# Third layer's query layout, reciprocals and one block's transposes in a four-layer decoder trunk

## The chip, the cores and the metric

The kernel runs on one core of a Trainium2 chip. The metric is the time of one execution on the device in microseconds; the lower, the better. Five engines work side by side, each through its own queue in order: TensorE (PE in the profile; its weight loads are PEld), VectorE (DVE), ScalarE (ACT), GpSimd (POOL) and SyncE (SP), which here only issues DMAs.

## The reference

Four decoder layers over one residual stream of 256 tokens by 1024 channels, all float32. Each layer adds a token mixer's output and then a squared-ReLU MLP's output to the stream, each behind an RMS norm. Layers 0 and 3 use differential attention, layer 1 block-sparse attention (with 256 tokens that is one causal block) and layer 2 sliding-window attention with sinks. What the change touches is layer 2, cut to what matters:

```python
qkv = h @ w_in + b_in                       # 1024 -> 16*64 (q) + 2*64 (k) + 2*64 (v)
q = apply_partial_rope(q.reshape(B, S, 16, 64), cos, sin) * 64 ** -0.5
s = einsum('bnqkgd,bnjkd->bnkgqj', qb, k2)  # 2 key heads, 8 query heads to each, 128 queries a block
s = where(band mask, s, -inf)               # a key is seen for 128 steps
m = maximum(max(s), sink)
e = exp(s - m)
p = e / (sum(e) + exp(sink - m))
o = einsum('bnkgqj,bnjkd->bnqkgd', p, v2)
return o @ w_out
```

Query head h and query head h + 8 belong to key heads 0 and 1.

## The kernel before

**Numbers as pairs.** Matmuls run in the fp32r type. A float32 operand is split into a high part (`whi`, `hg`, `uu`, `oo`: a copy into fp32r) and a low part (`wlo` and the second half of the others: the number less its high part), and three products out of four are summed. Weights come by DMA in pieces of 128x2048 (`fetch`, L173), and `stage` (L185) makes the pair of each: two copies of 128x1024 on ACT (L194) and two subtractions of 128x1024 on DVE (L195). Pieces are staged two ahead of use. Activations stay in the transposed layout (channels on partitions), the stream in `hT0` to `hT3`.

**A layer.** `mixer_layer` (L669) projects with `proj` into PSUM banks `p_in`, makes heads, and leaves the heads' outputs in `parts` (`oo`). `out_proj_all` (layers 0, 2, 3; tiles `p_d`) or `out_proj` (layer 1; tiles `p_d` and `p_e`) multiplies by the output weights and adds to the stream (`into`, L815), which also makes the next norm's pairs (`norm_part`, L345). `up_proj` (L866, tiles `p_up`) takes 16 weight pieces; for each, two banks are filled, copied out by ACT (`cross`, L812), added on DVE (`relu`, L813), squared (L890) and split (L892, L893). `down_proj` (tiles `p_down`, `p_last` in the last layer) closes the layer. In the first three layers, behind the second piece of `up_proj`, the norm's factor comes from GpSimd's sum over partitions (`row`, L387), a scaling (L393) and a DVE reciprocal of 128x256 (L1035).

**Layer 2's mixer.** Keys and values are projected first (L681). Then four pieces of query columns follow, c = 0 to 3. A piece holds 256 columns: two heads of the lower half and the two heads eight further on. Its columns lie lower half first, so that the eviction (L693 to L699) takes four DVE operations of 128x128 for a piece, each of which puts two heads into their places beside their partners in `qn`. After the rotary embedding (`rope`, L437) two blocks are run from a piece, each with one pair of heads; eight blocks in all, called 0 to 7 below. A block (`head_block`, L600) does:
- `scores` (L450): six matmuls into two banks `p_s`; four DVE operations that mask and negate and find the row maximum (`ns`, L473); four exponentials on ACT with row sums (`e` and `l`, L476), two more for the sinks (`es`, L479), and the sums added (L482);
- two DVE reciprocals (L606, L607) and one multiplication of 128x768 by them (L609);
- six transposes of 128x128 on TensorE against the identity (`p_t`, L137), copied to `et` by two ACT operations (L492);
- eight matmuls against the values (`p_av`), copied and split into `oo` (L621, L622).

Layer 1 uses the same `head_block`, and for four of its blocks `turned_aside` (L495): one DVE 32x32 transpose of 128x768 into `squares` (L500) and sixteen GpSimd copies of 32x192 (L504) that put the squares in place. There TensorE has no transposes for the block.

**What sets the order.** A scheduler orders each engine's queue. `TURNS` (L40) adds, by layer, pairs of TensorE instructions counted by tile name: the first of a pair is put behind the second in TensorE's queue. `behind` does the same for two instructions of any engine. PSUM tiles of the tag `wk` (`p_s`, `p_t`, `p_av`, `p_qk`, `p_up`) share four banks in turn, so a new one waits until the bank's last readers are done.

Of the kernel before, what the change touches and what calls it, by code (L numbers as in the profile page):

```python
# [19 lines left out]
P = 128  # L20
# [5 lines left out]
HD = 64  # L26
# [4 lines left out]
FAR = 5  # L31
WARM = 10
RAW = 4
ASIDE_HEADS = (0, 2)
ASIDE_PAIRS = (0,)
ASIDE = (0, 1, 2, 4)
# [49 lines left out]
    2: (  # L86
        (("p_qk", 0), ("p_in", 108)),
        (("p_s", 0), ("p_in", 149)),
        (("p_s", 12), ("p_in", 193)),
        (("p_av", 0), ("p_in", 227)),  # L90
        (("p_s", 36), ("p_d", 46)),
        (("p_s", 45), ("p_d", 60)),
        (("p_s", 42), ("p_d", 55)),
        (("p_d", 150), ("p_d", 161)),
    ),
    3: (
        (("p_s", 0), ("p_in", 83)),
# [54 lines left out]
def trunk(ctx: ExitStack, tc: tile.TileContext, xT, gains, lams, swa_row, fng, weights, out):  # L152
# [284 lines left out]
    def rope(x, nsub):  # L437

        ta = sb.tile([P, NT, nsub, 16], F32, tag="ropea", name="ropea")
        tb = sb.tile([P, NT, nsub, 16], F32, tag="ropeb", name="ropeb")  # L440
        V.tensor_tensor(ta, x[:, :, :, 0:16], cc[:, :, None, :].to_broadcast([P, NT, nsub, 16]), op=OP.mult)
        V.tensor_tensor(tb[:, :, :, 0:8], x[:, :, :, 8:16],
                        nsn[:, :, None, :].to_broadcast([P, NT, nsub, 8]), op=OP.mult)
        V.tensor_tensor(tb[:, :, :, 8:16], x[:, :, :, 0:8],
                        sn[:, :, None, :].to_broadcast([P, NT, nsub, 8]), op=OP.mult)
        V.tensor_tensor(x[:, :, :, 0:16], ta, tb, op=OP.add)

    scored, turned = [0], [0]

    def scores(q, k, mask, sinks):  # L450


        p0, p1 = bank("wk", "p_s0"), bank("wk", "p_s1")
        (qh, ql), (kh, kl) = q, k
        for p, t, n in ((p0, 0, P), (p1, 1, S)):
            o = p[:, :2 * n].rearrange("p (h m) -> p h m", h=2)
            a = slice(P * t, P * t + P)
            mm3(o, qh[:, a], ql[:, a], kh[:, :, :n], kl[:, :, :n], True, True)
        out = []
        if sinks is not None:  # L460
            es = tiny.tile([P, 2 * NT], F32, tag="es", name="es", bufs=2)
        scored[0] += 1
        pair_e = room(4 + scored[0] % 2, [P, 2, 3 * P], "e")
        ls = tiny.tile([P, 2 * NT], F32, tag="l", name="l", bufs=5)
        for c in range(2):
            ns = sb.tile([P, 3 * P], F32, tag="ns", name="ns", bufs=2)
            nm = tiny.tile([P, NT], F32, tag="nm", name="nm", bufs=4)
            l = ls[:, NT * c:NT * c + NT]
            e = pair_e[:, c]
            mk = mask[:, :, :].rearrange("p a b -> p (a b)")  # L470
            for t, p, n in ((0, p0, P), (1, p1, S)):
                s = slice(0, P) if t == 0 else slice(P, 3 * P)
                V.tensor_tensor_reduce(ns[:, s], p[:, n * c:n * c + n], mk[:, s], op0=OP.add, op1=OP.min,  # L473
                                       scale=-1.0, scalar=3.0e38 if sinks is None else sinks[c][1],
                                       accum_out=nm[:, t:t + 1])
                A.activation(e[:, s], ns[:, s], AF.Exp, bias=nm[:, t:t + 1], scale=-1.0,  # L476
                             accum_out=l[:, t:t + 1])
            if sinks is not None:
                A.activation(es[:, NT * c:NT * c + NT], nm, AF.Exp, bias=sinks[c][0])  # L479
            out.append((e, l))  # L480
        if sinks is not None:
            V.tensor_tensor(ls, ls, es, op=OP.add)  # L482
        return out, pair_e, ls
# [11 lines left out]
    def turned_aside(pair_e, h):  # L495

        turned[0] += 1
        ts = room((6, 7, 12, 13)[turned[0] % 4], [P, 2, 3 * P], "et")
        z = room(16 + h % 2, [P, 2, 3 * P], "squares")
        V.transpose(z.rearrange("p c m -> p (c m)"), pair_e.rearrange("p c m -> p (c m)"))  # L500
        to, at = (x.rearrange("p c (j i m) -> p (c j) i m", j=3, m=32) for x in (ts, z))
        for g in range(4):
            for i in range(4):
                G.tensor_copy(to[32 * i:32 * i + 32, :, g, :], at[32 * g:32 * g + 32, :, i, :])  # L504
        return [ts[:, i] for i in range(2)]
# [94 lines left out]
    def head_block(parts, q, k, v, mask, sinks, b, aside=False):  # L600

        _, both_e, l = scores(q, k, mask, sinks)

        rl = tiny.tile([P, 2, 3], F32, tag="rl3", name="rl3")
        l = l.rearrange("p (c t) -> p c t", c=2)
        V.reciprocal(rl[:, :, 0:2], l)  # L606
        V.reciprocal(rl[:, :, 2:3], l[:, :, 1:2])  # L607
        e = both_e.rearrange("p c (j m) -> p c j m", j=3)
        V.tensor_tensor(e, e, rl[:, :, :, None].to_broadcast([P, 2, 3, P]), op=OP.mult)  # L609
# [12 lines left out]
        V.tensor_tensor(both[:, 1], p[:, :S], f(both[:, 0]), op=OP.subtract)  # L622
        parts.append(both)
# [45 lines left out]
    def mixer_layer(i, n):  # L669
# [4 lines left out]
        if mixer == 2:  # L674
# [8 lines left out]
            for t in range(NT):  # L683
                V.scalar_tensor_tensor(kv[:, t, :], p[t], r[:, t:t + 1], rest[:, :256],
                                       op0=OP.mult, op1=OP.add)
            rope(kv[:, :, 0:P].rearrange("p t (s e) -> p t s e", e=HD), 2)
            put_k(kpad, turn(lambda b, t: kv[:, t, 0:P], 1), 1, False)
            kT = [x[:, 0] for x in kpad]
            first, second = [], []
            for c in range(4):  # L690
                p = proj(n, (256, 1), False, first)
                qn = room(c % 2, [P, NT, 256], "qn")
                for t in range(NT):  # L693
                    for h in range(2):
                        s = slice(P * h, P * h + P)
                        o = qn[:, t, :].rearrange("p (b h e) -> p b h e", h=2, e=HD)[:, :, h, :]
                        bs = bias[:, 512 * h + P * c:512 * h + P * c + P]
                        V.scalar_tensor_tensor(o, p[t][:, s].rearrange("p (b e) -> p b e", e=HD), r[:, t:t + 1],
                                               bs.rearrange("p (b e) -> p b e", e=HD), op0=OP.mult, op1=OP.add)  # L699
# [14 lines left out]

                first, second = [lambda f=block: f(0)], [lambda f=block: f(1)]
# [132 lines left out]
    def out_proj(parts, n, rest):  # L848
# [197 lines left out]
    T.take_turns(tc)  # L1046


def weight_pieces(arr):

    out = []
# [4 lines left out]
    for i in range(DEPTH):  # L1056
# [68 lines left out]
```

## Time and profile before

| | us |
|---|---|
| median of 3 runs | 1127.28 |
| lowest and highest run | 1126.79, 1131.32 |
| the profiled execution | 1127.19 |
| its span, first to last instruction | 1125.4 |
| PE busy | 1118.3 |
| PE weight loads busy | 974.8 |
| DVE busy | 840.3 |
| ACT busy | 652.3 |
| POOL busy | 136.6 |

The span is what the profile shows from the first to the last instruction; 1.79 us of the execution lie outside it. A matmul's end is modelled in this profile and matmuls overlap, so single durations of PE are longer than the time from one to the next; the chain of waits, which merges matmuls in order of time, gives their pace. Layer 2's mixer and output projection lie between 581 and 657 us, layer 1's `up_proj` between 403 and 492 us.

### The profile page before, as it was taken

What the parts mean: (1) busy time and instruction counts of PE and PEld (TensorE: products, weight loads), DVE (VectorE), ACT (ScalarE), POOL (GpSimd) and SP (SyncE); (2) the same over time, 40 slices, a digit from 0 to 9 for tenths busy, and PEclk for the clock granted to TensorE, in tenths of its full rate; (3) what the DMA queues carried; (4) which work ended last, traced back from release to release, by engine and by line L of the source; (5) the groups of instructions that cost most, each with busy time, mean ns of one, the idle gap of its engine ahead of it and who ended that gap; (6) DMA issues with size and microseconds to landing.
All of it is one profiled execution on the core that took longest, in us unless ns stands there. A gap on an engine that the chain in (4) does not pass through costs nothing.

```text
span 1125.4 us, 17122 instructions
## 1 busy us (share of the span) xinstructions
PE 1118.3 (99%) x6478; PEld 974.8 (87%) x6478; DVE 840.3 (75%) x1609; ACT 652.3 (58%) x1183; POOL 136.6 (12%) x273
## 2 busy tenths in 40 slices
PE   9999999999999999999999999999999999999997
PEld 7889888888888888888899998888888899888886
DVE  8888977656687798766569888765568788878453
ACT  7776666544476666554446765554446676555342
POOL 2250000000145200000000000000012410002800
PEclk9999999999999999999999999999999999999999
DMA  9533555555544446555563346555554444654551
GB/s 331 203 132 132 191 208 195 191 188 188 178 159 150 149 152 223 189 187 188 187 211 113 113 151 225 187 187 188 187 187 150 154 146 153 221 188 169 187 187 38
DMA packets 30466, 198.67 MB, mean 177 GB/s; under 512 B 3504, under 2 KB 5040, under 8 KB 7216
## 3 DMA queue, kind: packets, MB, share of 16 engines
q1 hardware_dynamic: 30096, 197.09, 50.6%
q8 instruction: 51, 0.84, 0.3%
q10 hardware_dynamic: 288, 0.49, 0.1%
q14 instruction: 31, 0.25, 0.1%
HBM read 196.52 MB, written 1.05 MB: 176 GB/s over the span
## 4 chain that ended last, share of the span: by engine, by line
PE 97%; DVE 1%; issue 1%; DMA 0%; SPq 0%; ACT 0%; POOLq 0%; POOL 0%; DVEq 0%
PE p_up L134 32%; PE p_down L134 24%; PE p_in L134 19%; PE p_last L134 7%; PE p_d L134 7%; PE p_s L134 3%; PE p_av L134 2%; PE p_qk L137 1%; PE p_t L137 1%; PE p_e L134 1%; DMA raw<-in_weights 0%; DVE wlo L195 0%; PE p_o L137 0%; DVE hg L352 0%; DVE acc L361 0%
## 5 line engine op out<-in xcount | busy, mean ns | idle before, releaser
L195 DVE TENSOR_TENSOR wlo<-raw,whi 128x1024 fp32r<-128x1024 f32 (+1 forms) x374 | 451.1, 1219 | 180.6 <-ACT whi L194 180.1
L194 ACT ACTIVATE whi<-raw 128x1024 fp32r<-128x1024 f32 (+1 forms) x374 | 383.8, 1045 | 200.3 <-issue 112.9
L134 PE MATMUL p_up<-hg,whi 128*128 128x512 f32 x1024 | 355.2, 394 | 0.0
L134 PE MATMUL p_up<-hg,wlo 128*128 128x256 f32 x1024 | 283.0, 277 | 0.0
L134 PE MATMUL p_down<-uu,whi 128*128 128x512 f32 x768 | 266.4, 394 | 0.0
L134 PEld LDWEIGHTS p_up<-hg,whi 128*128 128x128 f32 x1024 | 191.8, 188 | 44.0
L134 PE MATMUL p_down<-uu,wlo 128*128 128x256 f32 x768 | 212.7, 277 | 0.0
L134 PE MATMUL p_in<-whi,hg 128*128 128x512 f32 (+1 forms) x736 | 211.3, 370 | 0.0
L134 PEld LDWEIGHTS p_up<-hg,wlo 128*128 128x128 f32 x1024 | 192.3, 188 | 0.4
L134 PEld LDWEIGHTS p_down<-uu,whi 128*128 128x128 f32 x768 | 144.0, 188 | 33.4
L134 PEld LDWEIGHTS p_in<-whi,hg 128*128 128x128 f32 x736 | 132.3, 189 | 24.0 <-DVE hg L352 1.2
L134 PEld LDWEIGHTS p_down<-uu,wlo 128*128 128x128 f32 x768 | 144.2, 188 | 0.0
L134 PE MATMUL p_in<-wlo,hg 128*128 128x512 f32 (+1 forms) x368 | 130.1, 368 | 0.1
L892 ACT ACTIVATE uu<-u 128x512 fp32r<-128x512 f32 x64 | 40.4, 632 | 80.2 <-DVE u L890 80.2
L134 PE MATMUL p_d<-oo,whi 128*128 128x256 f32 (+1 forms) x416 | 85.2, 296 | 0.0
L134 PE MATMUL p_last<-whi,uu 128*128 128x512 f32 (+1 forms) x264 | 79.4, 383 | 0.0
L134 PEld LDWEIGHTS p_in<-wlo,hg 128*128 128x128 f32 x368 | 68.8, 189 | 11.5 <-DVE wlo L195 0.5
L812 ACT ACTIVATE cross<-p_up 128x256 f32<-128x256 f32 x128 | 47.9, 374 | 35.5 <-PE p_up L134 34.1
L134 PEld LDWEIGHTS p_d<-oo,whi 128*128 128x128 f32 x416 | 66.3, 191 | 1.9 <-issue 0.2
L351 ACT ACTIVATE hg<-hT,gn 128x256 fp32r<-128x256 f32 x64 | 31.4, 503 | 60.5 <-DVE hT L825 60.5
L476 ACT ACTIVATE e<-ns,nm 128x128 f32<-128x128 f32 (+1 forms) x128 | 56.8, 446 | 13.8 <-DVE nm L473 13.8
L518 POOL MEMSET kpadh<- 64x512 f32 x8 | 4.2, 521 | 494.3 <-PE p_down L134 494.1
(179 smaller groups left out, 1235.1 us busy)
## 6 DMA issues: line engine op xcount, KB each, us to landing
raw<-in_weights SPq DMA_DIRECT2D x181, 1024.0 KB, 4.9
raw<-in_weights SPq DMA_DIRECT2D x8, 256.0 KB, 4.8
raw<-in_weights SPq DMA_DIRECT2D x4, 512.0 KB, 7.0
hT<-in_xT SPq DMA_DIRECT2D x8, 128.0 KB, 4.7
bias<-in_swa_row SPq DMA_DIRECT2D x1, 512.0 KB, 4.2
grow<-in_fng SPq DMA_DIRECT2D x1, 512.0 KB, 3.8
lv<-in_lams SPq DMA_DIRECT2D x1, 256.0 KB, 6.6
out<-given ACTq DMA_DIRECT2D x1, 256.0 KB, 2.7
```

The lines of the kernel that those rows point to most:

```text
L134: return self.keep(out.tensor.name.rstrip("_0123456789"), self.engine.matmul(out, *args, **kw))
L137: return self.keep(out.tensor.name.rstrip("_0123456789"), self.engine.transpose(out, *args, **kw))
L194: high = A.activation(hi[:, s], raw[:, s], AF.Copy)
L195: low = V.tensor_tensor(lo[:, s], raw[:, s], f(hi[:, s]), op=OP.subtract)
L351: A.activation(both[:, 0], h, AF.Copy, scale=g)
L476: A.activation(e[:, s], ns[:, s], AF.Exp, bias=nm[:, t:t + 1], scale=-1.0, accum_out=l[:, t:t + 1])
L518: G.memset(f(kpad[x][HD * (1 - h):HD * (1 - h) + HD, :, h, :]), 0.0)
L812: A.activation(cross, p[:, S:], AF.Copy)
L892: A.activation(both[:, :, 0], r3(2)(u), AF.Copy)
```

## The change

1. **Query columns by head pairs.** The host lays the query weights and their bias out so that a head of the lower half and its partner stand side by side (`by_pairs`). A piece's eviction is then two DVE operations of 128x256, and in the first piece they are put behind the keys' rotary embedding.
2. **One reciprocal a block** in layer 2. The row sums go to two fixed tiles of 128x32 that are set to 1 at the start; an operand that reads the second and third value twice lets one reciprocal of 128x8 write all the factors.
3. **Block 4 of layer 2** (the fifth) is turned by `turned_aside`, in the block's own step.
4. **Turns.** Layer 2's list of turns is written anew (56 entries for 8), layer 1 gets two more. In the built program TensorE's order differs from before in few places: block 4's six transposes are gone; three output-projection matmuls stand earlier, ahead of block 5's transposes; one matmul of block 4's scores stands a little later; in the last output-projection piece of layer 2 the order of `p_d1` and `p_d3` is changed; and in layer 1 the last four matmuls of `up_proj`'s first piece stand behind five more of the second piece than before.
5. **Layer 1's last output tile** (`p_e` of the fourth) takes its high-weight product as two matmuls of 128x256 instead of one of 128x512, eight times.
6. `turned_aside` takes the two `squares` buffers the other way round.

The scheduler moves some DVE and ACT instructions with this. In layer 1's `up_proj`, the norm factor's scaling and reciprocal stand ahead of the first `relu` addition instead of behind it. In layer 2, ACT has the two copies of a block's transposes behind the next block's exponentials, and DVE has another order around blocks 4 to 7.

```diff
+ASIDE_THIRD = (4,)
...
 TURNS, layer 1:
         (("p_s", 18), ("p_in", 144)),
+        (("p_up", 28), ("p_up", 41)),
+        (("p_up", 30), ("p_up", 29)),
...
+    sink_sums = [cst.tile([P, 32], F32, name=f"sums{x}") for x in range(2)]
+    for x in sink_sums:
+        G.memset(x, 1.0)
...
-        ls = tiny.tile([P, 2 * NT], F32, tag="l", name="l", bufs=5)
+        if sinks is None:
+            ls = tiny.tile([P, 2 * NT], F32, tag="l", name="l", bufs=5)
+        else:
+            ls = sink_sums[scored[0] % 2][:, :2 * NT]
...
-        z = room(16 + h % 2, [P, 2, 3 * P], "squares")
+        z = room(17 - h % 2, [P, 2, 3 * P], "squares")
...
-        rl = tiny.tile([P, 2, 3], F32, tag="rl3", name="rl3")
-        l = l.rearrange("p (c t) -> p c t", c=2)
-        V.reciprocal(rl[:, :, 0:2], l)
-        V.reciprocal(rl[:, :, 2:3], l[:, :, 1:2])
+        rl = tiny.tile([P, 2, 4], F32, tag="rl3", name="rl3")
+        if sinks is None:
+            l = l.rearrange("p (c t) -> p c t", c=2)
+            V.reciprocal(rl[:, :, 0:2], l)
+            V.reciprocal(rl[:, :, 2:3], l[:, :, 1:2])
+        else:
+            V.reciprocal(rl.rearrange("p c (a b) -> p c a b", a=2),
+                         bass.AP(tensor=l.tensor, offset=l.offset, ap=[l.ap[0], [NT, 2], [1, 2], [1, 2]]))
         e = both_e.rearrange("p c (j m) -> p c j m", j=3)
-        V.tensor_tensor(e, e, rl[:, :, :, None].to_broadcast([P, 2, 3, P]), op=OP.mult)
+        V.tensor_tensor(e, e, rl[:, :, :3, None].to_broadcast([P, 2, 3, P]), op=OP.mult)
         es = [both_e[:, c] for c in range(2)]
-        yield
-        ets = turned_aside(both_e, b) if aside else transposed(es)
+        if aside and sinks is not None:
+            ets = turned_aside(both_e, b // 2)
+            yield
+        else:
+            yield
+            ets = turned_aside(both_e, b) if aside else transposed(es)
...
                 for t in range(NT):
-                    for h in range(2):
-                        s = slice(P * h, P * h + P)
-                        o = qn[:, t, :].rearrange("p (b h e) -> p b h e", h=2, e=HD)[:, :, h, :]
-                        bs = bias[:, 512 * h + P * c:512 * h + P * c + P]
-                        V.scalar_tensor_tensor(o, p[t][:, s].rearrange("p (b e) -> p b e", e=HD), r[:, t:t + 1],
-                                               bs.rearrange("p (b e) -> p b e", e=HD), op0=OP.mult, op1=OP.add)
+                    made = V.scalar_tensor_tensor(qn[:, t, :], p[t], r[:, t:t + 1], bias[:, 256 * c:256 * c + 256],
+                                                  op0=OP.mult, op1=OP.add)
+                    if c == 0:
+                        behind(tc, made.ins, roped.ins)
...
-                        h,
+                        h, h in ASIDE_THIRD,
...
+        if "H" in which:
+            for h in range(2):
+                T.matmul(r3(2)(p)[:, h], hi, x[:, h], start=start and h == 0, stop=False, skip_group_check=True)
...
-                    block_step(p, hi[:, k, P * b:P * b + P], lo[:, k, P * b:P * b + P], parts[k], k == 0, k == 7)
+                    block_step(p, hi[:, k, P * b:P * b + P], lo[:, k, P * b:P * b + P], parts[k], k == 0, k == 7,
+                               "Hl" if j and b else "hl")
...
+def by_pairs(x):
+    return np.moveaxis(x.reshape(*x.shape[:-1], 2, 8, HD), -3, -2).reshape(x.shape)
...
+            q = by_pairs(wi[:, :1024])
             for c in range(4):
-                rows(np.concatenate([wi[:, 512 * h + P * c:512 * h + P * c + P] for h in range(2)], axis=1))
+                rows(q[:, 256 * c:256 * c + 256])
```

More of the change, by code (lines that the diff above doesn't have):

```diff
@@ L84 @@
         (("p_s", 18), ("p_in", 144)),
-    ),
-    2: (
-        (("p_qk", 0), ("p_in", 108)),
[L88 to L94, printed above, removed]
+        (("p_up", 28), ("p_up", 41)),
+        (("p_up", 30), ("p_up", 29)),
+    ),
+    2: (
+        (("p_in", 109), ("p_qk", 1)),
+        (("p_qk", 2), ("p_in", 141)),
+        (("p_in", 142), ("p_qk", 5)),
+        (("p_s", 0), ("p_in", 149)),
+        (("p_in", 150), ("p_s", 11)),
+        (("p_t", 0), ("p_in", 185)),
+        (("p_qk", 6), ("p_t", 5)),
+        (("p_in", 186), ("p_qk", 9)),
+        (("p_s", 12), ("p_in", 193)),
+        (("p_in", 194), ("p_s", 16)),
+        (("p_s", 14), ("p_in", 195)),
+        (("p_in", 196), ("p_s", 17)),
+        (("p_t", 6), ("p_in", 199)),
+        (("p_in", 200), ("p_t", 11)),
+        (("p_s", 18), ("p_in", 203)),
+        (("p_in", 204), ("p_s", 23)),
+        (("p_t", 12), ("p_in", 223)),
+        (("p_in", 224), ("p_t", 17)),
+        (("p_av", 0), ("p_in", 227)),
+        (("p_qk", 10), ("p_av", 7)),
+        (("p_in", 228), ("p_qk", 13)),
+        (("p_s", 24), ("p_in", 236)),
+        (("p_in", 237), ("p_s", 28)),
+        (("p_d", 0), ("p_in", 239)),
+        (("p_t", 18), ("p_d", 3)),
+        (("p_d", 4), ("p_t", 20)),
+        (("p_s", 26), ("p_d", 5)),
+        (("p_t", 21), ("p_s", 29)),
+        (("p_s", 30), ("p_t", 23)),
+        (("p_d", 6), ("p_s", 32)),
+        (("p_s", 33), ("p_d", 11)),
+        (("p_d", 12), ("p_s", 35)),
+        (("p_av", 8), ("p_d", 38)),
+        (("p_qk", 14), ("p_av", 15)),
+        (("p_d", 39), ("p_qk", 17)),
+        (("p_s", 36), ("p_d", 46)),
+        (("p_d", 47), ("p_s", 40)),
+        (("p_t", 24), ("p_d", 49)),
+        (("p_d", 50), ("p_t", 26)),
+        (("p_s", 38), ("p_d", 52)),
+        (("p_t", 27), ("p_s", 41)),
+        (("p_d", 53), ("p_t", 29)),
+        (("p_s", 42), ("p_d", 55)),
+        (("p_d", 56), ("p_s", 44)),
+        (("p_s", 45), ("p_d", 60)),
+        (("p_d", 61), ("p_s", 47)),
+        (("p_t", 30), ("p_d", 87)),
+        (("p_av", 16), ("p_t", 35)),
+        (("p_d", 88), ("p_av", 23)),
+        (("p_t", 36), ("p_d", 91)),
+        (("p_av", 24), ("p_t", 41)),
+        (("p_s", 17), ("p_s", 14)),
+        (("p_s", 41), ("p_s", 38)),
+        (("p_qk", 0), ("p_in", 108)),
+        (("p_s", 29), ("p_s", 26)),
+        (("p_s", 45), ("p_d", 59)),
@@ L445, in rope @@
                         sn[:, :, None, :].to_broadcast([P, NT, nsub, 8]), op=OP.mult)
-        V.tensor_tensor(x[:, :, :, 0:16], ta, tb, op=OP.add)
+        return V.tensor_tensor(x[:, :, :, 0:16], ta, tb, op=OP.add)
     scored, turned = [0], [0]
+    sink_sums = [cst.tile([P, 32], F32, name=f"sums{x}") for x in range(2)]
+    for x in sink_sums:
+        G.memset(x, 1.0)
     def scores(q, k, mask, sinks):
@@ L685, in mixer_layer @@
                                        op0=OP.mult, op1=OP.add)
-            rope(kv[:, :, 0:P].rearrange("p t (s e) -> p t s e", e=HD), 2)
+            roped = rope(kv[:, :, 0:P].rearrange("p t (s e) -> p t s e", e=HD), 2)
             put_k(kpad, turn(lambda b, t: kv[:, t, 0:P], 1), 1, False)
@@ L1109 @@
         "lams": np.stack([arr("diff_lam_" + x) for x in ("q1", "k1", "q2", "k2")]),
-        "swa_row": np.concatenate([arr("swa_b_in")[0], arr("swa_sinks")[0]]),
+        "swa_row": np.concatenate([by_pairs(arr("swa_b_in")[0][:1024]), arr("swa_b_in")[0][1024:], arr("swa_sinks")[0]]),
         "fng": arr("final_norm_g"),
```

## The prediction

> **What bounds the kernel now.** I read the page's busy times first, then the chain of work that ended last, then the busy times by stretch, and only then single instructions.
>
> ```profile
> PE 1118.3 (99%) x6478; PEld 974.8 (87%) x6478; DVE 840.3 (75%) x1609; ACT 652.3 (58%) x1183; POOL 136.6 (12%) x273
> PE 97%; DVE 1%; issue 1%; DMA 0%; SPq 0%; ACT 0%; POOLq 0%; POOL 0%; DVEq 0%
> ```
>
> TensorE is busy for 99% of the span, and the chain back from the last instruction stays on it for 97%. The next view is of stretches; its columns are length, then busy time and count of PE, PEld, DVE, ACT and POOL, then clock, DMA share and GB/s.
>
> ```profile
> 0.00:18.75 18.75, 17.70 (x74) 13.73 (x74) 14.13 (x38) 13.91 (x25) 5.23 (x28) 1.00 0.85 290
> 581.00:620.80 39.80, 39.80 (x323) 38.21 (x322) 35.43 (x113) 24.98 (x66) 0.00 (x0) 1.00 0.39 133
> 620.80:655.40 34.60, 34.60 (x290) 32.09 (x289) 26.51 (x80) 26.63 (x72) 0.00 (x0) 1.00 0.33 117
> 1032.20:1125.40 93.20, 87.18 (x396) 72.47 (x395) 46.43 (x56) 32.20 (x38) 32.29 (x66) 0.98 0.40 138
> ```
>
> In both halves of layer 2's mixer PE has no idle time at all (39.80 of 39.80 and 34.60 of 34.60), although DVE there is busy for 89% and 77%. All that PE idles lies in the first and the last stretch, which the change does not reach: 1.05 and 6.02 us. So relief for DVE or ACT in layer 2 is worth nothing by itself. The time changes by what PE's own queue loses or gains in work, by the very short waits between its matmuls, and by new waits.
>
> **The change part by part.** PE's rows first, from the chain of waits (start, length, instructions); the last column is a count.
>
> ```profile
> 392.37 11.09 PE p_e L134 x64
> 599.02 0.62 PE p_qk L137 x4
> 607.72 0.44 PE p_qk L137 x4
> 627.59 0.66 PE p_t L137 x6
> 634.97 0.69 PE p_s L134 x3
> 635.66 3.23 PE p_d L134 x27
> 638.89 0.66 PE p_t L137 x6
> 639.55 1.45 PE p_av L134 x16
> ```
>
> *Block 4's six transposes.* They are the row at 627.59 and leave PE: **-0.66**. The two ACT copies behind them go as well; ACT has idle time and is worth nothing here.
>
> *The eviction of queries.* The four transposes of the first piece's queries take 0.62, those of the second 0.44, because the first wait for the rotary embedding:
>
> ```profile
> 598.98 0.42 PEld L137 LDWEIGHTS p_qk<-ident,qn 128*128 128x128 f32 x4 [0.16 <-DVE qn L446]
> L698 DVE SCALAR_TENSOR_TENSOR qn<-p_in,nr,bias 128x128 f32<-128x128 f32 x16 | 4.8, 343 | 1.0 <-PE p_in L134 1.0
> L684 DVE SCALAR_TENSOR_TENSOR rest<-p_in,nr,rest 128x256 f32<-128x256 f32 x2 | 0.9, 478 | 0.0
> ```
>
> Four operations of 343 ns become two of a shape that L684 shows at 478 ns: 1.37 - 0.96 = 0.41 us of DVE a piece. For the first piece this comes ahead of the transposes and covers their wait: **-0.16**. For the other pieces PE waits for nothing that DVE does there, so it is worth nothing; if it did not come, nothing would be lost either.
>
> *One reciprocal.* It saves the shorter of two small DVE operations in each block (0.13 us in the rows below), off PE's path: 0. The two memsets of 128x32 at the start stand in GpSimd's queue, which is busy for 5.23 of the first 18.75 us: 0. The exchange of the `squares` buffers keeps the same distance between uses: 0.
>
> *Layer 1's split product.* A pair of 128x512 and 128x256 takes 11.09 / 32 = 0.347; a 128x256 with its own weights 3.23 / 27 = 0.120. Three of these make 0.359, so each of the eight splits adds 0.012: **+0.10**. Nothing starts earlier for it: ACT's copy reads the same half, which is finished one matmul before the end either way.
>
> *Layer 1's up projection.* The stretch behind it is not covered by the rows above, so these come from the timeline (start, length, engine):
>
> ```profile
> 405.73 0.63 PE L134 MATMUL p_up<-hg,whi 128*128 128x512 f32 x2
> 408.86 0.69 PE L134 MATMUL p_up<-hg,whi 128*128 128x512 f32 x2
> 414.49 0.39 PE L134 MATMUL p_up<-hg,whi 128*128 128x512 f32 x1
> ...
> 408.51 0.48 DVE L352 SCALAR_TENSOR_TENSOR hg<-hT,gn,hg 128x256 fp32r<-128x256 f32 x1 [0.58 <-ACT hg L351]
> 410.18 0.42 DVE L813 TENSOR_TENSOR relu<-p_up,cross 128x256 f32<-128x256 f32 x1
> 412.18 0.29 DVE L393 TENSOR_SCALAR row<-row 128x256 f32<-128x256 f32 x1 [1.58 <-POOL row L387]
> 412.51 1.75 DVE L1035 RECIPROCAL row<-row 128x256 f32<-128x256 f32 x1
> 414.18 0.36 DVE L813 TENSOR_TENSOR relu<-p_up,cross 128x256 f32<-128x256 f32 x1
> ```
>
> Two like matmuls take 0.69 instead of 0.63 at 408.86, where they meet the last `hg` (408.51 to 408.99). The new turns put five matmuls (0.87 us) in between: **-0.06**. But in the built program DVE now has `row` and its reciprocal ahead of the first `relu`. That `relu` frees the bank of the third piece's first matmul, and the built program has this matmul wait for it. It moves from 410.18 to the place of the second one, 414.18 to 414.54, and PE wants the bank at 414.49. The split product pushes both by 0.10, the wait that went pulls PE alone by 0.06; with some 0.05 for a signal (DVE's gaps between dependent steps) PE waits 414.64 + 0.05 - 414.53 = **+0.15**, between 0 and 0.3. The second `relu` is then 0.3 later, but its bank is wanted 16 matmuls on.
>
> *Block 6's transposes.* PE wants them at 638.89, 0.64 after the multiplication that they wait for has ended. Now PE comes 0.66 + 0.16 earlier, and DVE's order there has changed.
>
> ```profile
> 326.00 1.09 DVE L609 TENSOR_TENSOR e<-e,rl 128x768 f32<-128x768 f32 x1
> 635.37 1.22 DVE L195 TENSOR_TENSOR wlo<-raw,whi 128x1024 fp32r<-128x1024 f32 x1
> 636.51 0.15 DVE L482 TENSOR_TENSOR l<-l,es 128x4 f32<-128x4 f32 x1
> 636.58 0.48 DVE L473 CUSTOM_DVE_ANT_0 ns<-p_s,band,rest 128x256 f32<-128x256 f32 x1
> 637.08 0.14 DVE L607 RECIPROCAL rl<-l 128x2 f32<-128x2 f32 x1
> 637.13 0.33 DVE L473 CUSTOM_DVE_ANT_0 ns<-p_s,band,rest 128x128 f32<-128x128 f32 x1
> 637.38 0.95 DVE L609 TENSOR_TENSOR e<-e,rl 128x768 f32<-128x768 f32 x1
> 638.25 0.48 DVE L473 CUSTOM_DVE_ANT_0 ns<-p_s,band,rest 128x256 f32<-128x256 f32 x1
> ```
>
> Before, DVE did a weight half (L195) while PE ran block 7's last scores (634.97 to 635.66), and the last `ns` came behind the multiplication. Now a `ns` of 128x256 comes first and so waits for those scores, and the last `ns` comes ahead of the multiplication. From the end of the scores, by distances from start to start above: 0.41 + 1.14 + 0.07 + 0.25 + 0.09 + 0.41 + 0.87 = 3.24, so 638.90 on before's clock, where PE is at 638.89: the slack of 0.64 is just gone. Both shift together, since the count begins at a matmul. GpSimd now copies beside DVE; such a multiplication took 1.09 instead of 0.95 in layer 1, twice in this count. With a signal that makes **+0.3**, between 0 and 0.9 (all of PE's 0.82 lead given back).
>
> *Block 4's turn on DVE and GpSimd.* Neither is in layer 2's rows, so layer 1's stand for them.
>
> ```profile
> 323.38 29.96 POOL L504 COPY et<-squares 32x192 f32<-32x192 f32 x48 [18.90 <-DVE squares L500]
> 364.09 8.53 POOL L504 COPY et<-squares 32x192 f32<-32x192 f32 x16 [10.76 <-DVE squares L500]
> L500 DVE STREAM_TRANSPOSE squares<-e x4: 964/968/975, 322.3 to 363.0; 128x768 f32<-128x768 f32 x4
> L504 POOL COPY et<-squares x64: 333/343/1379, 323.4 to 372.3; 32x192 f32<-32x192 f32 x64
> 626.07 0.95 DVE L609 TENSOR_TENSOR e<-e,rl 128x768 f32<-128x768 f32 x1
> ```
>
> The block's multiplication ends at 627.0 as before (what DVE saves, a weight half that now stands ahead of it takes); one `ns` (0.41) and the transpose (0.97) follow, so GpSimd starts at 628.4. Sixteen copies took 8.53 in one case and 29.96 / 3 = 9.99 in the others: ready at 637.0 to 638.4. PE wants them for `p_av` at 639.55 - 0.82 + 0.3 = 639.0. Hidden, with 0.6 to 2.0 to spare: 0. If that cover is gone, PE waits with everything behind it in its queue: the rest of `p_av`, block 7's transposes and the projection.
>
> *The tail of layer 2's projection.* DVE now has the third norm part later, at about 656.3, by its rows' lengths; PE reads it behind 657.17 in before's clock: 0.
>
> **Sum.** -0.66 - 0.16 + 0.10 - 0.06 + 0.15 + 0.3 = -0.33. Against the profiled execution, 1127.19 (1125.4 and 1.79 around it), this is 1126.9. That execution lies 0.09 below the median of the three runs, so I leave it at 1126.9.
>
> **The rivals.** *DVE takes all of it back.* Block 6's wait is 0.9 and the bank's 0.3: -0.78 + 1.2 = +0.42, 1127.6. For it: DVE's order there is worse and its chain is 3.24 long without a gap. Against: its start hangs on a matmul that also comes earlier.
>
> *GpSimd's copies come late (slower than before).* A copy takes 0.34 alone, 1.2 to 1.4 beside a DVE operation with two operands in SBUF (L195, L609), and five of these follow in the 10.6 us until PE needs the result. From 10.6 us on, each microsecond is one of PE's: with 12 us, the time is 1126.9 + 1.4 = 1128.3; with every copy at 1.24, 19.8 us and 1136. For it: the same copies' longest, 1379 ns. Against: 48 of them, with DVE as busy, kept to 9.99 a block. The Trainium skill's page "SBUF — State Buffer", section "SBUF: two separate sides", says that such a DVE operation and a GpSimd operation that reads SBUF take turns at one port pair, each for its whole length. The 1379 ns against 343 agree with it.
>
> *PE is not the bound.* Then six transposes fewer bring nothing: 1127.2. The Trainium skill's page "Perfetto Trace Analysis", section "Identifying the Most-Contended Engine", calls matmul busy time a bad measure and weight-load time a good one; by that, 87%, PE would have headroom and the term would be 0 instead of -0.66. Against: the 27 matmuls behind 635.66 start 0.120 apart without a gap, and six transposes take 0.66 from the next matmul's start.
>
> **How the numbers follow.** The forecast has 0.62, DVE taking it back 0.18, late copies 0.13 (0.03 of it far beyond), PE not the bound 0.07. About 0.5%, 5.6 us, is what a measurement of this kernel can tell from no change. Everything that could be gained here adds up to 0.88, so faster by more has 0.01; slower by more needs late copies at almost their worst or a wait that I have not seen: 0.04; within 0.5%: 0.95. The range goes from all waits at nothing (-0.78, 1126.4), less the 0.5 by which the lowest run lay under the median, to late copies at 12 us with half a microsecond for the runs: 1125.9 to 1128.8.
>
> **What would show it.** Right: layer 2's PE rows stay without idle time but for one short wait ahead of block 6's transposes for `e` (L609's line), and the stretch from the second piece's start to the last `p_d` is some half a microsecond shorter; a wait of 0.1 to 0.2 at the third piece of layer 1's `up_proj` for `relu`; `p_e` takes 11.19. Wrong: PE idle for POOL ahead of `p_av`, idle time above 0.5 for DVE in layer 2, or a start and an end that differ from before, since I give them no change.

## The result and the profile after

| | before | after |
|---|---|---|
| median of 22 runs each, us | 1127.57 | 1131.06 |
| lowest and highest run | 1126.79, 1131.86 | 1127.84, 1133.04 |
| the profiled execution | 1127.19 | 1130.95 |
| its span | 1125.4 | 1129.1 |

The ratio after to before is 1.002, with a 95% interval of 1.0011 to 1.0028: slower by 0.1 to 0.3%, less than the half per cent that the prediction counted as no change, but outside its range. The medians tell only part of it, because the runs of either kernel fall into two groups with nothing between 1129.0 and 1130.6. Of before's 22 runs, 15 lie around 1127.2 and 7 around 1131.0; of the changed kernel's, 4 lie around 1128.15 and 18 around 1131.1. So two things want explaining: 0.9 us inside a group, and why most runs went to the upper one. Both profiles are typical: before's is of its lower group, the changed kernel's of its upper one.

The page of the changed kernel, busy times and chain:

```profile
PE 1120.7 (99%) x6480; PEld 975.4 (86%) x6480; DVE 841.1 (74%) x1594; ACT 651.7 (58%) x1181; POOL 145.1 (13%) x291
PE 97%; DVE 1%; issue 1%; DMA 0%; SPq 0%; ACT 0%; POOLq 0%; POOL 0%; DVEq 0%
```

TensorE is the bound as before. The same four stretches, shifted to where their work now stands, show new idle time on it in one place only outside the start: 33.77 busy of 34.60 in the second half of layer 2's mixer.

```profile
0.00:18.75 18.75, 17.18 (x75) 13.51 (x76) 14.38 (x39) 13.37 (x25) 5.38 (x31) 1.00 0.86 297
584.30:624.10 39.80, 39.80 (x323) 38.15 (x322) 35.10 (x102) 25.20 (x66) 0.00 (x0) 1.00 0.39 136
624.10:658.70 34.60, 33.77 (x280) 30.95 (x280) 26.80 (x73) 25.38 (x68) 8.91 (x16) 1.00 0.32 112
1035.73:1129.13 93.40, 87.38 (x398) 72.67 (x396) 46.50 (x56) 32.30 (x38) 32.23 (x66) 0.99 0.40 139
```

To see where 3.73 us of span went, take the first matmul of each tile name as a landmark in both timelines, and subtract lengths from landmark to landmark:

| from | to | before | after | difference |
|---|---|---|---|---|
| start | layer 1's `p_e` | 392.21 | 392.06 | -0.15 |
| `p_e` | layer 1's `p_up` | 11.09 | 11.18 | +0.09 |
| layer 1's `p_up` | layer 2's `p_in` | 177.58 | 180.96 | **+3.38** |
| `p_in` | first group of `p_av` | 35.62 | 35.64 | +0.02 |
| first group of `p_av` | second group | 11.68 | 10.96 | **-0.72** |
| second group | third group | 11.30 | 12.31 | **+1.01** |
| third group | layer 2's `p_up` | 15.74 | 15.89 | +0.15 |
| `p_up` | end | 470.18 | 470.13 | -0.05 |

(TensorE runs `p_av`, the product with the values, two blocks at a time, in four groups. Block 4's transposes stood ahead of the second, block 6's stand ahead of the third, which also holds block 4's `p_av`.)

Layer 1's MLP, to which the change adds no work, holds nearly all of it. PE is never idle there, and the granted clock is 1.00 in both kernels. The count tells the story: how many matmuls (the first number in brackets) fall into the same 140 us, first before, then after.

```profile
430.00:570.00 140.00, 140.00 (x809) 122.46 (x808) 94.71 (x127) 71.92 (x102) 0.00 (x0) 1.00 0.55 190
```

```profile
430.00:570.00 140.00, 140.00 (x794) 121.32 (x793) 94.08 (x127) 72.16 (x101) 0.00 (x0) 1.00 0.55 188
```

794 for 809: every pair (one matmul of 128x512, one of 128x256) takes 1.9% longer. "PE busy" is blind to that, since busy is 140.00 of 140.00 in both. The single starts show a rhythm. Before, the pairs take 0.347 us each. In the changed kernel a pattern of three pairs repeats, 1.060 long, 0.3533 a pair, from one point on to the end of the MLP. That point, in the timeline of weight loads of the changed kernel:

```profile
414.50 0.19 PEld L185 LDWEIGHTS p_up<-hg,whi 128*128 128x128 f32 x1 [0.25 <-DVE relu L882]
...
414.84 0.19 PEld L185 LDWEIGHTS p_up<-hg,whi 128*128 128x128 f32 x1
...
415.20 0.19 PEld L185 LDWEIGHTS p_up<-hg,whi 128*128 128x128 f32 x1
...
415.55 0.19 PEld L185 LDWEIGHTS p_up<-hg,whi 128*128 128x128 f32 x1
...
415.90 0.19 PEld L185 LDWEIGHTS p_up<-hg,whi 128*128 128x128 f32 x1
```

The first row is the third piece's weight load, waiting for `relu`: the wait that the prediction had priced at 0.15. Ahead of it the pairs took 0.347; from the second load shown on, three pairs take 415.90 - 414.84 = 1.06. The wait itself cost some 0.2. The pace behind it, kept for about 480 pairs at 0.0067 more, cost 3.2.

The other wait is the one ahead of block 6's transposes, 0.83 us of idle time. The chain of waits there, in order of time:

```profile
638.53 0.03 issue
638.56 0.48 DVE ns L531
639.04 0.01 DVE nm L531
639.05 1.30 DVE wlo L246
640.35 0.22 DVE sums L540
640.57 0.26 DVE ns L531
640.84 0.01 DVE nm L531
640.84 0.12 DVE rl L669
640.96 0.35 DVE ns L531
641.31 0.01 DVE nm L531
641.32 0.87 DVE e L672
642.19 0.15 DVE sums L540
642.34 0.84 PE p_t L188 x6
```

### The profile page after: what moved, and what is told of

It is laid out like the page before. It is cut to its first block, busy times and chain, and to the rows that moved or that the text cites. A ratio compares the mean times of both kernels' runs of the same rounds, so it can differ in the third digit from the quotient of the medians.

```text
span 1129.1 us, 17134 instructions
## 1 busy us (share of the span) xinstructions
PE 1120.7 (99%) x6480; PEld 975.4 (86%) x6480; DVE 841.1 (74%) x1594; ACT 651.7 (58%) x1181; POOL 145.1 (13%) x291
## 3 DMA queue, kind: packets, MB, share of 16 engines
HBM read 196.52 MB, written 1.05 MB: 175 GB/s over the span
## 4 chain that ended last, share of the span: by engine, by line
PE 97%; DVE 1%; issue 1%; DMA 0%; ACT 0%; SPq 0%; POOLq 0%; POOL 0%; DVEq 0%
PE p_up L185 32%; PE p_down L185 24%; PE p_in L185 19%; PE p_last L185 7%; PE p_d L185 7%; PE p_s L185 3%; PE p_av L185 2%; PE p_qk L188 1%; PE p_t L188 1%; PE p_e L185 1%; DVE wlo L246 0%; DMA raw<-in_weights 0%; PE p_o L188 0%; DVE hg L403 0%; ACT whi L245 0%
```

## The experiments

All of them stand beside runs of the kernel before on the same chip: e5 to e8 on one chip, the others on a second. So a comparison across the two chips goes by each run's distance from before's lower group beside it, where that matters. "Lower" and "upper" count runs below and above 1129.6 us. The last column is the length from layer 1's first `p_up` to layer 2's first `p_in` in the profile of that kernel, 177.6 at 0.3467 a pair and 181.0 at 0.3533.

| run | median | lower (their median) | upper | MLP of layer 1 |
|---|---|---|---|---|
| after | 1131.06 | 4 (1128.15) | 18 | 180.96 |
| e1 no turns | 1130.93 | 4 (1127.92) | 8 | 181.07 |
| e2 no split | 1131.12 | 0 | 11 | 180.99 |
| e3 before + turns | 1130.74 | 0 | 11 | 180.99 |
| e4 before + split | 1130.80 | 2 (1128.09) | 10 | 181.07 |
| e5 neither | 1128.09 | 9 (1127.84) | 3 | 177.59 |
| e6 DVE order | 1130.01 | 1 (1126.80) | 11 | 177.76 |
| e7 one reset | 1128.53 | 9 (1128.42) | 3 | 180.94 |
| e8 no waits | 1126.79 | 10 (1126.78) | 1 | 177.51 |
| e9 wait in layer 2 | 1131.55 | 0 | 5 | 177.58 |
| e10 before, no waits | 1127.31 | 10 (1127.24) | 1 | 177.50 |
| e11 thirteen resets | 1128.97 | 8 (1128.58) | 3 | 178.38 |
| e12 block 4 on TensorE | 1127.57 | 10 (1127.53) | 1 | 177.51 |
| e13 no waits, sinks later | 1126.58 | 11 (1126.58) | 1 | 177.55 |
| e14 before, sinks later | 1127.35 | 9 (1127.19) | 3 | 180.86 |

Before itself, in the result and beside all of these: 142 runs, 110 lower and 32 upper.

**Which edit?** The first theory (R) was that the turns alone did it, by the wait for `relu`.

```diff
-        (("p_up", 28), ("p_up", 41)),
-        (("p_up", 30), ("p_up", 29)),
```


> The changed kernel without layer 1's two new turns. What is known: in the changed kernel's profile the matmul pairs of layer 1's whole MLP (408 to 581 us) take 0.3533 us instead of 0.3467, from the weight load on that waited 0.25 us for the first relu of up_proj's third piece. Theory R (that wait sets the slower rhythm, and nothing breaks it until the MLP ends): DVE's order is the old one without the turns, the wait is gone, layer 1's pairs take 0.3467, the median is 3.3 to 3.5 lower, about 1127.7. Rival S (the eight split matmuls ahead set the rhythm): layer 1 stays at 0.3533, median about 1131. Rival C (the rhythm is a matter of chance in each run, whatever the edit): both values, in proportions that no edit moves.

```diff
-                    block_step(p, hi[:, k, P * b:P * b + P], lo[:, k, P * b:P * b + P], parts[k], k == 0, k == 7,
-                               "Hl" if j and b else "hl")
+                    block_step(p, hi[:, k, P * b:P * b + P], lo[:, k, P * b:P * b + P], parts[k], k == 0, k == 7)
```


> The changed kernel with layer 1's last output tile as before (one matmul of 128x512, not two of 128x256, eight times). Theory R: the wait for relu stays, so does the slow rhythm in most runs; median 1130.8 to 1131.0 (the 0.10 of the eight splits comes off). Rival S: layer 1's pairs take 0.3467, median about 1127.6. Rival C: a mixture as without the edit.

e3 is before with the two turns that e1 takes out, e4 before with the split that e2 takes out.

> The kernel before, with layer 1's two new turns and nothing else. Theory R: DVE has the norm factor's reciprocal ahead of the first relu, the third piece's weight load waits for it, and layer 1's pairs take 0.3533 in most runs: median 1130.6 to 1130.9 against 1127.5. Rival S: no such wait matters, median 1127.5 within 0.2. Rival C: as before's own mixture.

> The kernel before, with the split of layer 1's last output tile and nothing else. Theory R: DVE keeps the old order, no wait, pairs at 0.3467; median 1127.6 (0.10 more). Rival S: pairs at 0.3533 in most runs, median 1130.8. Rival C: as before's own mixture.

All four medians are at 1130.7 to 1131.1. Theory R fails at e1 and e4, rival S (the split) at e2 and e3: **each edit alone is enough**. Rival C, chance that no edit moves, fails too: 6 of these 46 runs are lower, and 28 of the 35 of before beside them. In the profiles of e1 and e4 there is again a wait, ahead of the same rhythm, but another one; this is e4's:

```profile
408.73 0.19 PEld L134 LDWEIGHTS p_up<-hg,whi 128*128 128x128 f32 x1 [0.25 <-DVE hg L352]
```

It is the wait for the last `hg`, which cost 0.06 before. The built program says why it grew: with the split, the scheduler puts one 128x512 matmul (0.23 us) of the second piece behind the last four of the first, so TensorE asks for that `hg` 0.23 earlier. So the theory became W: any such wait, just ahead of a long unbroken run of pairs, may set the slower rhythm.

> The changed kernel with both of layer 1's edits undone (no new turns, no split product); layer 2 as changed. Each edit alone left layer 1's MLP in the slower rhythm (0.3533 us a pair) in the runs so far: the split by a weight load that waited 0.25 for the last hg, the turns by one that waited 0.25 for relu. Theory W (any wait of that length on a weight load ahead of the MLP's unbroken run of pairs sets the slower rhythm, and it lasts until the MLP ends): with neither edit only before's short wait is left, so the times are shared as before's are (four in five in the lower group), the lower group near 1127.5 and the profile's pairs at 0.3467. Rival L (layer 2's part of the change shifts something for the whole program): most runs stay near 1130.8.

9 of 12 runs lower, and 177.59: with both edits undone layer 1 is where before is. The lower group is 0.7 above before's beside it (1127.84 against 1127.10), which is layer 2's part. Rival L is out.

**Is it layer 1's place?** e9 puts a wait into layer 2's `up_proj` of the kernel before; on DVE the first `relu` goes behind a low weight half:

```diff
+    behind(tc, relus[2, 0, 0], halves[109, 0])
```


> The kernel before, with one constraint: in layer 2's up_proj the first relu stands behind the first low half of weight piece 109 on DVE, so that it ends near 670.2 where TensorE wants the bank at about 669.4. Nothing of layer 1 is touched. Theory W (a wait ahead of an unbroken run of pairs sets the slower rhythm wherever it is): a wait of 0.5 to 1.0 us at the third piece, and pairs at 0.3533 in layer 2's MLP behind it in most runs, about 480 pairs or 3.2 us: median 1131.0 to 1131.5, and a lower group near 1128.0. Rival P (it is a matter of layer 1's place in the program): only the wait itself is paid, most runs at 1127.8 to 1128.3.

```profile
670.90 0.50 PE L134 MATMUL p_up<-hg,whi 128*128 128x512 f32 x1 [0.95 <-DVE relu L815]
```

Layer 1's MLP is at 177.58 in this profile. Layer 2's `up_proj` takes 92.19 instead of 89.53, 2.7 more for a wait of 1.0, and its pairs are at 0.3533 behind the wait to the MLP's end; five runs of five are upper, at 1.0037 (1.0025 to 1.005) of before. Rival P is out: a wait ahead of layer 2's MLP does what the others do in layer 1.

**Can the rhythm be broken?** In the fifth piece of layer 1's `up_proj`:

```diff
+            if T.layer == 1 and g == 4:
+                steps[7:10] = [(order[7 + x], w) for x, w in ((0, "h"), (1, "h"), (0, "l"), (2, "h"), (1, "l"), (2, "l"))]
```


> The changed kernel; in layer 1, in the fifth piece of up_proj, three pairs of matmuls have their order changed from high low high low high low to high high low high low low, as the first piece has it already. No matmul is added, no wait is touched. Theory W: the rhythm is a state of the queue that such an order breaks (in the first piece every profile goes over to 0.3467 behind it), so pairs take 0.3533 from the relu wait to there (some 50 pairs, 0.3 us) and 0.3467 behind it: median about 1128.1. Rival D (the pace belongs to the data's place, the code or the clock of that stretch): 0.3533 comes back at once, median 1131.

9 of 12 runs are lower, for 4 of 22 without it, and their median is some 0.3 above the changed kernel's lower one, as the 39 pairs from the wait to there at 0.0067 should make it. No wait was touched and no work removed, so the rhythm is a state that the order of three pairs can end, and rival D fails in these nine runs. But the profiled run is an upper one: there the new order fell on another place of the pattern of three, and the slower rhythm was back five pairs later. e11 has it in all pieces from the fourth on (`g > 2`).

> The changed kernel; in layer 1, the order high high low high low low for three pairs in every piece of up_proj from the fourth on, thirteen times, not once as in the run before it (which left 3 of 12 runs in the upper group, the profiled one among them, in which the slower rhythm came back within five pairs). If each such place ends the slower rhythm in some three of four cases and does not start it: the upper group is gone, all runs between 1127.7 and 1128.5. If it starts it as often as it ends it: times anywhere between 1128 and 1131.

The second expectation came out: times are spread from 1128.05 to 1130.9, and in the profile the pace changes from piece to piece. The single starts show all thirteen places: six fell into the slower rhythm, and each ended it; seven fell into the faster pace, and six of these started the slower one. Where it ended the rhythm it fell behind one of the shorter of the three intervals (0.350), in e7's profile behind the longest (0.361). So such an order ends the rhythm or starts it, by where it falls. It is no remedy.

**Taking the waits away.** e6 puts the low half of weight piece 104 behind block 6's multiplication, nothing else:

```diff
+    behind(tc, halves[104, 1], mults[6])
```


> The changed kernel with one constraint more: in layer 2 the second low half of weight piece 104 stands behind block 6's multiplication on DVE instead of ahead of it. The wait of 0.82 us ahead of block 6's transposes should go, and no later one should take its place (block 7's transposes are wanted 2.8 later, its multiplication would end some 1 us ahead): 0.8 to 0.9 less than the changed kernel in each group of times. Layer 1 is as it was, so most runs near 1130.1, the rest near 1127.2. Rival: the low half, 2 us later, is now what the projection's next piece waits for, and nothing or less than half is won.

The upper group falls from 1131.10 to 1130.03 (by 0.9 when each is taken against before's upper group beside it), and in the profile the second group of `p_av` to the third takes 11.36 instead of 12.31: the wait had cost 0.95, and no later wait came. The profile also holds the best evidence on the rhythm. It caught the one lower run of twelve, and it has the same wait for `relu` as the changed kernel:

```profile
414.51 0.19 PEld L185 LDWEIGHTS p_up<-hg,whi 128*128 128x128 f32 x1 [0.25 <-DVE relu L886]
...
414.85 0.19 PEld L185 LDWEIGHTS p_up<-hg,whi 128*128 128x128 f32 x1
...
415.20 0.19 PEld L185 LDWEIGHTS p_up<-hg,whi 128*128 128x128 f32 x1
...
415.55 0.19 PEld L185 LDWEIGHTS p_up<-hg,whi 128*128 128x128 f32 x1
...
415.89 0.19 PEld L185 LDWEIGHTS p_up<-hg,whi 128*128 128x128 f32 x1
```

```profile
430.00:570.00 140.00, 140.00 (x810) 123.44 (x809) 94.92 (x127) 71.77 (x101) 0.00 (x0) 1.00 0.55 190
```

Three pairs take 1.04, and 810 matmuls fit into the 140 us. The same wait at the same place gives either rhythm. Up to the third load the rows differ by 0.01 at most from one to the next; what decides can't be read from them.

e8 removes all waits found: the turns stay (no wait for `hg`), the split goes, the first `relu` stands ahead of the scaling on DVE, and e6's line is in. e10 does the layer 1 part of it to the kernel before.

```diff
+        if T.layer == 1:
+            behind(tc, made.ins, relus[1, 0, 0])
```


> The changed kernel with the new turns kept, the split product undone, the first relu of layer 1 put ahead of the norm factor's scaling on DVE (as before had it), and block 6's multiplication ahead of the low half of piece 104. Theory W: no weight load of layer 1's up_proj waits for hg (the turns) or for relu (the order), so no run falls into the slower rhythm, not even the one in five of before; block 6's wait is gone: median 1126.3 to 1126.7, against 1127.3. Rival L: most runs near 1130.

> The kernel before, with layer 1's two turns and the first relu ahead of the norm factor's scaling on DVE: in layer 1's up_proj the last hg is not waited for, and relu neither. Theory W: the upper group that one in five of before's runs falls into goes, lower group as before's or 0.06 lower; median 1127.1. Rival: that upper group has another cause; still one run in five near 1130.8. Against e8 it gives what layer 2's part of the change is worth without block 6's wait: by theory 0.6 to 0.8 for the transposes and the query rows.

One upper run in 11 in each. e8's median is 0.5 below before's, but the interval of the ratio, 0.9996 (0.9988 to 1.0005), includes no difference at all. That the upper group would vanish did not come true. Over all runs its share goes with the wait ahead of layer 1's MLP: 69 of 80 where a weight load waited 0.25 or longer (the changed kernel, e1 to e4, e6), 38 of 166 with the short wait for `hg` (before, e5, e14), 4 of 45 with neither (e8, e10, e12, e13). The first difference is far beyond chance; the second, 38 of 166 to 4 of 45, is at its edge. No profile caught one of those four.

e12 is e8 with block 4 back on TensorE (`ASIDE_THIRD = ()`, later `p_t` numbers in the turns raised by 6).

> The kernel without waits of e8, with block 4's six transposes back on TensorE (the turns that count p_t shifted by six for the later blocks). Theory: six transposes cost TensorE 0.66 us, and nothing of what GpSimd did is on the path: lower group 0.6 to 0.7 above e8's. Rival (TensorE has room there, as its weight-load share would say): the same time as e8 within 0.2.

The lower group is 0.75 above e8's, or 0.54 when each is taken against before's beside it; from the first group of `p_av` to the second, the profile has 11.61 for 10.96. In e12's chain the six transposes have the price that the prediction gave them:

```profile
628.37 0.66 PE p_t L188 x6
```

Last, the spread inside the lower group. In e8's profile TensorE waits 1.01 us at the start of layer 2, for an `hg` that ACT makes from `hT`. DVE makes that `hT` behind the sinks' negation, which waits for a row by DMA:

```profile
582.99 0.17 DVE L754 TENSOR_SCALAR rest<-rest 128x16 f32<-128x16 f32 x1 [4.07 <-DMA rest<-in_swa_row]
```

```profile
587.20 0.51 PE L185 MATMUL p_in<-whi,hg 128*128 128x256 f32 x2 [1.01 <-ACT hg L405]
```

The profiles with layer 1's MLP at the same length have that negation at 580.83 (before), 582.12 (e10), 582.81 (e12) and 582.99 (e8), and PE's wait for `hg` there at 0, 0.18, 0.46 and 1.01: it is a matter of when the row lands. e13 is e8 and e14 is before, with the negation behind the last `hg`:

```diff
+            behind(tc, made.ins, n.last)
```


> The version without waits of e8, with one constraint more: on DVE the negation of layer 2's sinks, which waits for a row by DMA, stands behind the last hg of the norm ahead, not in front of the low half of a weight piece. If the late row is what spreads the lower group: TensorE's wait of 1.0 us in e8's profile at the start of layer 2's projection is gone, the lower group lies within 0.6 us, and the median is 0.3 to 0.5 lower than e8's, near 1126.4. If it isn't: as e8, 1126.8.

> The kernel before with the same one constraint on the sinks' negation. If the late row spreads before's lower group too, its median falls by 0.1 to 0.3 to 1127.0 and its spread narrows to 0.6; the upper group (about one run in six) stays, since layer 1's wait for hg is still there. If not, no difference.

e13 has no wait of PE between the start and the end in its profile; its lower group is narrower (0.92 for 1.95 us) and 0.2 lower than e8's, half of what was expected. At 0.9981 of before (0.997 to 0.9992), 1126.58, it is the one version that beats both kernels clearly, though in that comparison 11 of before's 23 runs were upper ones; between the lower groups it is 0.5 ahead of before. For e14 the expectation failed: its lower group is neither lower than before's (1127.19 for 1127.12) nor narrower (0.99 for 0.89 us). So the late row is shown for e8's profile, and it does not spread before's lower group. e14's profile caught an upper run of a kernel whose layer 1 is that of before:

```profile
408.88 0.70 PE L134 MATMUL p_up<-hg,whi 128*128 128x512 f32 x2
409.42 0.28 PE L134 MATMUL p_up<-hg,wlo 128*128 128x256 f32 x1
```

```profile
430.00:570.00 140.00, 140.00 (x794) 121.45 (x793) 93.94 (x127) 72.19 (x101) 0.00 (x0) 1.00 0.56 188
```

The two matmuls at the wait for `hg` take 0.70 (0.69 in before's profile), and 794 matmuls fit into the 140 us. So the slower rhythm also makes an upper run where layer 1 is as before. That the short wait for `hg` sets it there is likely by the counts above, but not shown, and its length does not decide. e5's profile has the same two matmuls at 0.70 and the faster pace behind them:

```profile
408.89 0.70 PE L183 MATMUL p_up<-hg,whi 128*128 128x512 f32 x2
430.00:570.00 140.00, 140.00 (x809) 123.47 (x808) 94.68 (x127) 71.85 (x102) 0.00 (x0) 1.00 0.55 190
```

A wait for another engine is not needed either. In e13's profile the slower rhythm holds for 56 pairs, from layer 1's last projection pieces (386.4) to the exchanged order in the first piece of `up_proj` (405.8). The load ahead of them has a pause of 0.17, as in every profile, and waits for nothing that the profile shows. The 32 pairs of `p_e`, which lie inside, in the chains of e8 and of e13:

```profile
392.44 11.09 PE p_e L185 x64
392.23 11.31 PE p_e L185 x64
```

In all 16 profiles the pace goes with the group: 180.9 to 181.1 in layer 1's MLP (or the slower pace in layer 2's, e9) with every execution of 1130.36 us or more, 177.5 to 177.8 with every one of 1128.0 or less; e11's execution, with 178.38, took 1128.47.

## Why the prediction was wrong, step by step

*What bounds the kernel*: right. PE is 99% busy, and the 3.73 us of span were found on its queue.

*Layer 1's up projection, +0.15 between 0 and 0.3*: the wait was foreseen with its place, its cause on DVE and its length (some 0.2), and **this is the step that failed**: its price was taken as its length. Behind it stood 480 pairs without a break, and in 18 of 22 runs they ran in another rhythm, +3.2. The prediction had allowed for "the very short waits between its matmuls", but not for a wait that changes the pace of what follows. Before's three runs held a hint: one took 1131.32, 4 us above the other two, beyond the top of the range, and no term stood for it.

*Layer 1's split product, +0.10*: the row came out to the digit,

```profile
392.22 11.19 PE p_e L185 x72
```

but the same thing failed here: the split also moves a matmul at the last `hg`, and that wait alone does the same (e4). *The wait for `hg`, -0.06*: gone with the turns, as said; layer 1's MLP takes 177.50 in e10 for 177.58.

*Block 6's transposes, +0.3 between 0 and 0.9*: right in place and cause, mis-sized: 0.95, just outside its bounds. This alone turns the forecast's gain into a loss, and it is one of the prediction's own signs of being wrong, idle time above 0.5 for DVE in layer 2. DVE's chain from the scores took 638.53 to 642.19, 3.66 for 3.24. The weight half took 1.30 from start to start for 1.14 and the sums 0.22 for 0.07. Both read two operands from SBUF while GpSimd copied. The Trainium skill's page "SBUF — State Buffer", section "SBUF: two separate sides", has such an operation and a GpSimd operation that reads SBUF take turns at a shared pair of ports, and these two rows agree with it.

*Six transposes, -0.66*: right (e12). With them the rival that PE is not the bound is gone. The Trainium skill's page "Perfetto Trace Analysis", section "Identifying the Most-Contended Engine", judges TensorE's headroom by the share of weight loads, among others. By their 86% there would be some; here six transposes cost their full 0.65.

*The eviction of queries, -0.16*: did not come.

```profile
602.34 0.63 PE p_qk L188 x4
```

0.63 for 0.62. On DVE the first piece's evictions take 0.79 instead of 1.05 from start to start, but they now stand behind the keys' rotary embedding instead of between its steps, and the keys' part takes 1.51 instead of 1.25. From there to the next weight half it is 2.30 in both kernels, so nothing came earlier.

*GpSimd's copies, 0*: right.

```profile
631.79 9.54 POOL L562 COPY et<-squares 32x192 f32<-32x192 f32 x16 [48.63 <-DVE squares L558]
```

Done at 641.33, and wanted for `p_av` at 643.18, or at 642.2 without block 6's wait: 0.9 to spare, where 0.6 to 2.0 was said. The rival of late copies is out.

*The tail of layer 2's projection, 0*: from the third group of `p_av` to `p_up` it took 15.84 to 15.90 in every version with layer 2's change, and 15.73 to 15.75 in every one without (before, e3, e4, e9, e10, e14). Between single starts of the two profiles, 0.06 of it lies inside the last `p_av` group and 0.08 where the last projection piece, whose order changed, goes from one `p_d` bank to the next. Why they are longer was not settled.

By its own terms the forecast -0.33 becomes +0.5: block 6 at 0.95 instead of 0.3, no 0.16, 0.15 at the tail, 0.2 instead of 0.15 for `relu`, less 0.1 to 0.2 of small gains at the start and elsewhere. The two profiles agree: of their 3.73, 3.2 are the rhythm. The lower groups lie further apart, 1128.15 (four runs) against 1127.19; the other 0.4 was not traced. The upper group is the rhythm on top. The rival "DVE takes all of it back" was the nearest, at 1127.6, and by the mechanism in layer 2 it was right; the rhythm was in no rival.

## What to carry to other kernels

Where a saturated TensorE runs hundreds of like matmuls without a break, price a new short wait ahead of them not by its length alone but also by what the pace behind it may become; count matmuls in a window of fixed length to see the pace, as busy time doesn't show it. When times fall into two groups, ask of each profile which group its run belongs to before two profiles are compared. A turn in one engine's queue that removes a wait of 0.06 must be followed through the other engines' order, which the scheduler then changes.

## What the runs showed of the hardware that was not expected

Pairs of a 128x512 and a 128x256 matmul with a weight load each hold either of two average paces for as long as nothing interrupts them: 0.3467 us, or 0.3533 in a pattern of three pairs, 1.9% apart, at a granted clock of 1.00 in both. A wait ahead changes how often it is the slower one: 69 of 80 runs with a load that waited 0.25 or longer, 38 of 166 with before's shorter wait. It does not settle it by its length, since the same rows lead to either (0.25 in the changed kernel and in e6, 0.70 in e14 and in e5). Another order of three pairs can take it from either to the other (e7, e11). What in the engine makes the pattern was not found, nor what sent one run in 11 or 12 of e8, e10, e12 and e13 to the upper group.
